# Attention stage: the mixer gates' steps given out two at a time, six matmuls of 512 columns in a row instead of three

## The chip, the core and the metric

The kernel runs on one core of a Trainium2 chip. The core has five engines with a queue of instructions each: TensorE (PE in the profile, with its weight loads shown apart as PEld), VectorE (DVE), ScalarE (ACT), GpSimd (POOL) and SyncE (SP), which starts most of the DMAs. Operands lie in the on-chip memory SBUF, matmul results in PSUM, which has eight banks of 512 float32 columns on 128 partitions. The metric is device time in microseconds (us) from start to end of one execution.

## The reference

One layer of a decoder trunk with two token mixers side by side, whose outputs are weighed by gates; 1024 tokens of 1024 values, float32.

```python
h = rmsnorm(x, norm_mix[layer])
(q, kc, vc, ks, vs, kw, vw, nsa_g, rq, rk, rv, rg, gate_a, gate_b) = jnp.split(
    h @ w_in[layer], offsets, axis=-1)
...
nsa_out = nsa_batched(q, kc, vc, ks, vs, kw, vw, nsa_g.reshape(B, S, NSA_HEADS, 3), ...)
ret_out = (jax.nn.silu(rg.astype(jnp.float32)) * ret.reshape(B, S, RET_W)).astype(x.dtype)
mix = (jax.nn.sigmoid(gate_a) * (nsa_out @ w_proj_a[layer])
       + jax.nn.sigmoid(gate_b) * (ret_out @ w_proj_b[layer]))
x = x + mix @ w_out[layer]
h = rmsnorm(x, norm_mlp[layer])
x = x + jnp.square(jax.nn.relu(h @ w_up[layer])) @ w_down[layer]
return rmsnorm(x, norm_final)
```

`nsa_mixer` is the attention: 8 query heads in 2 groups, and three branches for each query block of 128 tokens (compressed keys, selected blocks of 64 keys, all 16 of which are taken at this length, and a window of 512 keys), each with a softmax of its own and summed with gates.

## The kernel before

The kernel goes through stages: norm and projections, retention, attention, output projection, MLP. The change lies in the attention stage, 357 to 742 us of the trace. The order of PE's instructions there is written by hand: PE runs them as the program gives them. The order on the other engines is made by a scheduler in the framework, from the program's order and what each instruction needs; only instructions marked with `keep_in_program_order` are held to it.

A float32 product is made of three matmuls: each operand is split into a high part (`wh`, `QQ`, `ph`; on ACT) and the rest (`wl`, `ql`, `pl`; a subtraction on DVE), and high by high, low by high and high by low are added up in PSUM.

The stage has 32 units: query blocks 7 down to 0, two groups each, two pairs of heads each. A unit's work is given out by generators, one piece at each call:

- `scores` (L1105 on): for each of the two heads the matmuls of the scores S over the selected keys (`KKs`), then over the window (`KKw`) with the compressed ones. Each group of up to 512 columns takes one of the four banks of the pool `psS`. DVE adds the mask and takes the extreme value `mx` (L1152, L1159), ACT the exponent (L1163) from the bank into `pSa`, `pSb` or `pW`, and then the bank is free. DVE makes the factors `cf` (L1168 to L1170) and POOL scales the weights (L1173).
- `pv`: for two blocks of keys at a time four transposes (L1232, L1233) into a `pt` bank, `ph` on ACT (L1234), `pl` on DVE (L1235), and, two groups later, the matmuls into O (`V`), with a bank of its own.
- `prep_q`: splits the next queries (L1097, L1098).

Between these lie the mixer gates (`gate_a`, `gate_b`): 32 half rows, made by `gate_pieces`. Each is eight steps of three matmuls of 512 columns (`gps<-bh,wh`, `gps<-bl,wh`, `gps<-bh,wl`) into one bank, with a `yield` behind each step; then ACT takes the bank (`gst`, L1059) and SP writes it out. At the sixth step `gate_w(i + 1)` asks for the next weight, once for two half rows: a DMA into `raw`, `wh` on ACT (L185) and `wl` on DVE (L188), 1024 columns each. The gps bank is one; from the seventeenth half row on every second one takes a bank of the pool of the scores instead.

What stands where is decided by a list of places. `place(it, n, lo, hi)` gives `n` pieces of a generator the midpoints of `n` equal parts of `lo` to `hi`, in units; the list is sorted by these numbers and run through. For the gates:

```python
        for n, k in enumerate(GATES):
            place(gate_it, k, n - 1, n)
```

`GATES` has the number of steps in each unit: 14, then 8 in sixteen units, 6 in twelve, 7 in the last four; together 242, and two more (`GATE0`) ahead of the first. The remaining 12 of the 256 steps come behind the stage.

Of the kernel before, what the change touches and what calls it, by code (L numbers as in the profile page):

```python
# [37 lines left out]
PH_B = 4  # L38
PS_B = 4
PS_S = 4  # L40
GATES = [14] + [8] * 16 + [6] * 12 + [7, 7, 7, 7]
S_BEG = 0.08
S_END = 0.6
W_AT = 0.7
# [69 lines left out]
def hybrid_block(ctx: ExitStack, tc: tile.TileContext, a: dict, out: bass.AP):  # L114
# [954 lines left out]
    def all_gates():  # L1069
        for n in range(32):  # L1070
            yield from gate_pieces(n)

    gate_it = all_gates()

    def gates(k=1):
        for _ in range(k):
            next(gate_it, None)

    with ExitStack() as e3:
# [13 lines left out]
        def prep_q(qb, g):  # L1093
            qt = qs[qb, g]
            QQ = at.tile([P, 4, P], F32R, name="QQ")
            ql = at.tile([P, 4, P], F32R, name="ql")
            A.activation(QQ, qt, AF.Copy)  # L1097
            V.tensor_sub(ql, qt, QQ)  # L1098
            qs[qb, g] = (QQ, ql)
            nxt = 2 * (7 - qb) + g + 2  # L1100
            if nxt < 16:
                load_q(7 - nxt // 2, nxt % 2)
            yield
# [150 lines left out]
        def n_scores(qb):  # L1254
            sel, win = (qb + 4) // 4, (min(qb + 1, 5) + 3) // 4 + (1 if qb == 3 else 0)
            return 2 * (sel + win)

        def n_pv(qb):
            return 2 * ((qb + 1 + min(qb + 1, 5) + 2) // 2)
# [9 lines left out]
        def place(it, n, lo, hi):  # L1269
            for k in range(n):  # L1270
                todo.append((lo + (hi - lo) * (k + 0.5) / n, len(todo), it))

        for n, (qb, g, hp) in enumerate(units):
            u = {}
            if hp == 0:
                if n:
                    place(prep_q(qb, g), 1, n - 1 + Q_AT - 1, n - 1 + Q_AT - 1)
            if n % 4 == 0:
                todo.append((n - 1 + S_BEG, len(todo), None, qb))
            it = scores(qb, g, hp, u)  # L1280
            ahead = SHORT if qb < 2 else 0.0
            place(it, n_scores(qb), n - 1 + S_BEG - ahead, n - 1 + S_END - ahead)
            place(it, 1, n - 1 + W_AT - ahead, n - 1 + W_AT - ahead)
            it = pv(qb, g, hp, u)
            place(it, n_pv(qb) - 1, n, n + 1 + V_END)
            last = 1.1 / n_pv(units[n + 1][0]) if n + 1 < nu else V_LAST
            place(it, 1, n + 1 + last, n + 1 + last)
        for n, k in enumerate(GATES):
            place(gate_it, k, n - 1, n)
        gates(GATE0)  # L1290
        next(prep_q(7, 0))
        todo.append((B_AT, len(todo), None, None))
# [754 lines left out]
```

## Time and profile before

| | |
|---|---|
| median of 3 runs | 1544.56 us (1544.07 to 1545.82) |
| profiled execution: span from first to last instruction | 1542.0 us |
| instructions in the span | 22621 |
| PE / DVE / ACT / POOL busy, of the span | 99% / 68% / 47% / 33% |
| chain of waits, share of PE | 89% |
| attention stage | 357 to 742 us |

The profile gives the span of one execution; the runs' time also has what lies ahead of the first and behind the last instruction, 2.6 us by the median. A row of a timeline has the start, the duration in us, the engine, the line, the operation and what it writes and reads, without the numbers of the buffers; in square brackets stands the idle time before it and what released it. The view by lines has the number, the busy time, the mean of one in ns and the idle time before. In the waits each row has the waiting and the releasing instruction, the us in all, the number of times and the longest.

### The profile page before, as it was taken

What the parts mean: (1) busy time and instruction counts of PE and PEld (TensorE: products, weight loads), DVE (VectorE), ACT (ScalarE), POOL (GpSimd) and SP (SyncE); (2) the same over time, 40 slices, a digit from 0 to 9 for tenths busy, and PEclk for the clock granted to TensorE, in tenths of its full rate; (3) what the DMA queues carried; (4) which work ended last, traced back from release to release, by engine and by line L of the source; (5) the groups of instructions that cost most, each with busy time, mean ns of one, the idle gap of its engine ahead of it and who ended that gap; (6) DMA issues with size and microseconds to landing.
All of it is one profiled execution on the core that took longest, in us unless ns stands there. A gap on an engine that the chain in (4) does not pass through costs nothing.

```text
span 1542.0 us, 22621 instructions
## 1 busy us (share of the span) xinstructions
PE 1529.9 (99%) x7841; PEld 1290.3 (84%) x7841; DVE 1044.4 (68%) x2044; ACT 719.1 (47%) x1602; POOL 514.3 (33%) x601
## 2 busy tenths in 40 slices
PE   9999999999999999999999999999999999999998
PEld 6888888898888888888888888888888888888887
DVE  6865661666877878776754378876666768786573
ACT  6653462555677777776421163222222244443452
POOL 4110011002333333343000014767777518723540
PEclk9999999999999999999999999999999999999999
DMA  6202215762111212111744433444444797673472
GB/s 208 88 18 65 59 45 131 204 177 68 58 35 42 62 42 62 48 56 62 233 137 157 137 126 104 154 151 150 150 150 150 242 344 265 207 238 123 143 269 100
DMA packets 101764, 202.87 MB, mean 132 GB/s; under 512 B 10698, under 2 KB 27346, under 8 KB 101586
## 3 DMA queue, kind: packets, MB, share of 16 engines
q1 hardware_dynamic: 100946, 199.33, 39.9%
q0 software_dynamic: 560, 1.84, 0.3%
q8 instruction: 62, 1.02, 0.3%
q14 instruction: 52, 0.43, 0.1%
q10 hardware_dynamic: 144, 0.26, 0.0%
HBM read 147.78 MB, written 53.61 MB: 131 GB/s over the span
## 4 chain that ended last, share of the span: by engine, by line
PE 89%; DVE 4%; issue 3%; ACT 2%; POOL 1%; DMA 1%; POOLq 0%; SPq 0%; ACTq 0%; DVEq 0%
PE mm L158 24%; PE mmu L158 20%; PE mmd L158 19%; PE gps L158 10%; PE S L158 4%; PE O L158 4%; PE pt L1233 2%; PE pt L1232 2%; PE pc L158 1%; PE pO L158 1%; ACT pW L1163 1%; PE pD L158 0%; PE tp L391 0%; PE pS L158 0%; DVE pl L1235 0%
## 5 line engine op out<-in xcount | busy, mean ns | idle before, releaser
L1387 DVE TENSOR_TENSOR wl<-raw,wh 128x1024 fp32r<-128x1024 f32 x134 | 220.5, 1670 | 91.3 <-ACT wh L1386 91.3
L1386 ACT ACTIVATE wh<-raw 128x1024 fp32r<-128x1024 f32 x134 | 136.7, 1054 | 159.4 <-PE mmd L158 112.3
L158 PE MATMUL mmd<-wl,wh 128*128 128x512 f32 (+1 forms) x464 | 177.2, 382 | 0.0
L158 PE MATMUL mmd<-wh 128*128 128x512 f32 (+1 forms) x464 | 177.2, 382 | 0.0
L158 PE MATMUL mmd<-wh,wl 128*128 128x512 f32 (+1 forms) x464 | 177.1, 382 | 0.0
L194 POOL TENSOR_SCALAR msq<-ssq 128x1 f32<-128x1 f32 (+1 forms) x32 | 7.5, 234 | 384.3 <-ACT h L200 219.6
L1235 DVE TENSOR_TENSOR pl<-pt,ph 128x512 fp32r<-128x512 f32 (+1 forms) x160 | 103.4, 648 | 40.4 <-ACT ph L1234 38.9
L158 PE MATMUL mm<-wh,bh 128*128 128x512 f32 (+1 forms) x320 | 122.4, 383 | 0.1
L158 PE MATMUL mm<-wl,bh 128*128 128x512 f32 (+1 forms) x320 | 118.9, 372 | 0.0
L158 PE MATMUL mm<-wh,bl 128*128 128x512 f32 (+1 forms) x320 | 118.0, 373 | 0.0
L1234 ACT ACTIVATE ph<-pt 128x512 fp32r<-128x512 f32 (+1 forms) x160 | 90.9, 569 | 54.0 <-PE pt L1233 53.0
L1152 DVE CUSTOM_DVE_ANT_0 S<-S,edge_m 128x352 f32<-128x352 f32 (+5 forms) x200 | 101.4, 514 | 13.9 <-PE S L158 10.3
L158 PE MATMUL gps<-bh,wh 128*128 128x512 f32 x256 | 107.8, 421 | 0.7 <-ACT gst L1059 0.6
L158 PEld LDWEIGHTS mmd<-wh 128*128 128x128 f32 x464 | 87.2, 188 | 17.1
L158 PEld LDWEIGHTS mmd<-wl,wh 128*128 128x128 f32 x464 | 87.2, 188 | 17.0
L158 PEld LDWEIGHTS mmd<-wh,wl 128*128 128x128 f32 x464 | 87.2, 188 | 16.7
L158 PE MATMUL mmu<-bh,wh 128*128 128x512 f32 (+1 forms) x264 | 101.0, 383 | 0.0
L158 PE MATMUL mmu<-bl,wh 128*128 128x512 f32 (+1 forms) x264 | 100.9, 383 | 0.0
L158 PE MATMUL mmu<-bh,wl 128*128 128x512 f32 (+1 forms) x264 | 100.6, 383 | 0.0
L158 PE MATMUL gps<-bl,wh 128*128 128x512 f32 x256 | 100.6, 393 | 0.0
L158 PE MATMUL gps<-bh,wl 128*128 128x512 f32 x256 | 100.5, 393 | 0.0
L1173 POOL TENSOR_SCALAR pSa<-pSa,cf 128x512 f32<-128x512 f32 (+3 forms) x64 | 38.9, 621 | 173.4 <-DVE mx L1159 63.5
(379 smaller groups left out, 4161.9 us busy)
## 6 DMA issues: line engine op xcount, KB each, us to landing
raw<-u_scr SPq DMA_DIRECT2D x56, 512.0 KB, 4.3
raw<-w_down SPq DMA_DIRECT2D x41, 512.0 KB, 5.1
raw<-w_up SPq DMA_DIRECT2D x32, 512.0 KB, 4.0
u_scr<-u SPq DMA_DIRECT2D x60, 256.0 KB, 4.2
u_scr<-s SPq DMA_DIRECT2D x45, 256.0 KB, 2.3
y<-w_down SPq DMA_DIRECT2D x16, 512.0 KB, 6.6
x<-x SPq DMA_DIRECT2D x8, 512.0 KB, 4.8
raw<-w_ga SPq DMA_DIRECT2D x8, 512.0 KB, 3.8
```

The source lines that it names most:

```text
L158: T.matmul(o, w, m, start=start, stop=stop)
L194: G.tensor_scalar(m[:, :w], ssq, 1.0 / n, EPS, op0=OP.mult, op1=OP.add)
L1152: r = V.tensor_tensor_reduce(sc, sc, mk, -0.125, BIGPOS, OP.add, OP.min, mx[:, i, b:b + 1])
L1163: A.activation(o, sc, AF.Exp, bias=mx[:, i, m:m + 1], scale=-1.0, accum_out=sums[:, i, b:b + 1])
L1173: G.tensor_scalar(v, v, cf[:, i, b:b + 1], 1.0, op0=OP.mult, op1=OP.mult)
L1232: T.transpose(tp[:, bi * 2], p0, ident)
L1233: T.transpose(tp[:, bi * 2 + 1], p1, ident)
L1234: A.activation(ph[:, :n], tp[:, :n], AF.Copy)
L1235: V.tensor_sub(pl[:, :n], tp[:, :n], ph[:, :n])
L1386: A.activation(h[:, :n], r, AF.Copy)
L1387: V.tensor_sub(l[:, :n], r, h[:, :n])
```

## The change

The gates' steps are given out two at a time. A new generator calls `gates(2)` for each piece, and half as many pieces are placed in each unit, so that each is six matmuls of 512 columns in a row, and there are half as many of them. For that the counts have to be even, and the last four of `GATES` become 8, 6, 8, 6; the sum stays 242.

```diff
-GATES = [14] + [8] * 16 + [6] * 12 + [7, 7, 7, 7]
+GATES = [14] + [8] * 16 + [6] * 12 + [8, 6, 8, 6]
...
+        def gate_rows():
+            while True:
+                gates(2)
+                yield
+
+        rows_it = gate_rows()
         for n, k in enumerate(GATES):
-            place(gate_it, k, n - 1, n)
+            place(rows_it, k // 2, n - 1, n)
```

What this moves on PE, in a unit of query block 5 behind the scores of the second head (the gap between the first head's selected score and the first window score `S<-KKw,QQ` has this piece and the like one of the head before in it):

```order
 L158 MATMUL S<-KKs,QQ 128x256
 L158 MATMUL S<-KKs,ql 128x256
-L158 MATMUL gps<-bh,wh 128x512
-L158 MATMUL gps<-bl,wh 128x512
-L158 MATMUL gps<-bh,wl 128x512
 L158 MATMUL O<-ph,VV 128x256
 L158 MATMUL O<-pl,VV 64x256 x2
```

The step that stood between the last selected score and the O matmuls is gone from there. It is now part of a row of six behind the first window score:

```order
 L158 MATMUL S<-KKw,QQ 128x352
 L158 MATMUL S<-KKw,ql 128x352
+L158 MATMUL gps<-bh,wh 128x512
+L158 MATMUL gps<-bl,wh 128x512
+L158 MATMUL gps<-bh,wl 128x512
+L158 MATMUL gps<-bh,wh 128x512
+L158 MATMUL gps<-bl,wh 128x512
+L158 MATMUL gps<-bh,wl 128x512
 L1232 MATMUL pt<-ident,pW 128x128
 L1233 MATMUL pt<-ident,pW 128x128
```

On DVE, at the end of a unit of query block 6 in which a gate weight is split (442 to 449 us of the trace of before), the rows before are:

```order
L1098 TENSOR_TENSOR ql_5512<-qt_4710,QQ_5511 128x512
L1168 TENSOR_TENSOR sums_4947<-sums_4947 128x2
L1169 RECIPROCAL cf_4949<-sums_4947 128x2x2
L1170 TENSOR_TENSOR cf_4949<-cf_4949,gts_89 128x2x2
L1235 TENSOR_TENSOR pl_5075<-pt_5073,ph_5074 128x512
L188 TENSOR_TENSOR wl_5088<-raw_5085,wh_5087 128x1024
L1235 TENSOR_TENSOR pl_5107<-pt_5105,ph_5106 128x256
L1235 TENSOR_TENSOR pl_5136<-pt_5134,ph_5135 128x512
```

and now, at the same place:

```order
L1235 TENSOR_TENSOR pl_5050<-pt_5048,ph_5049 128x512
L1168 TENSOR_TENSOR sums_4943<-sums_4943 128x2
L1169 RECIPROCAL cf_4945<-sums_4943 128x2x2
L1170 TENSOR_TENSOR cf_4945<-cf_4945,gts_89 128x2x2
L188 TENSOR_TENSOR wl_5079<-raw_5076,wh_5078 128x1024
L1235 TENSOR_TENSOR pl_5084<-pt_5082,ph_5083 128x512
L1235 TENSOR_TENSOR pl_5104<-pt_5102,ph_5103 128x256
L1098 TENSOR_TENSOR ql_5518<-qt_4716,QQ_5517 128x512
```

The subtraction of the gate weight, `wl`, has moved ahead of the second but last `pl` of the unit (`pl_5075` before, `pl_5084` now; the last one is of 256 columns), and the split of the next queries, `ql`, from before the factors to behind the last `pl`. On PE the consumers stand in this order now:

```order
L158 MATMUL gps_4961<-bh_85,wh_4670 128x512
L158 MATMUL gps_4961<-bl_86,wh_4670 128x512
L158 MATMUL gps_4961<-bh_85,wl_4671 128x512
L158 MATMUL O_4925<-pl_5050,VV_3667 64x256
L158 MATMUL O_4925<-ph_5049,VV_3667 128x256
L158 MATMUL O_4925<-pl_5050,VV_3667 64x256
L158 MATMUL O_4925<-ph_5049,VV_3667 128x256
L158 MATMUL O_4925<-pl_5084,VV_3667 64x256
L158 MATMUL O_4925<-ph_5083,VV_3667 128x256
```

The O matmuls of `pl_5084` follow those of `pl_5050` without a gate step between them; before, a step lay between these two groups of four.

## The prediction

> **What bounds the kernel now.** I read the page first, then the waits of the attention stage on TensorE, then the timeline of two places in it. The busy row, the slices and the row of clocks come first.
>
> ```profile
> PE 1529.9 (99%) x7841; PEld 1290.3 (84%) x7841; DVE 1044.4 (68%) x2044; ACT 719.1 (47%) x1602; POOL 514.3 (33%) x601
> PE   9999999999999999999999999999999999999998
> PEclk9999999999999999999999999999999999999999
> core 0: 1542.0 us, clock 0.999
> ```
>
> TensorE (PE) works from the first slice to the last, at a granted clock of 0.999, so the end is set by how much PE has to do and by the gaps in it. The view by stretches, for the attention stage alone (its columns: span, then busy time and instructions of PE, PEld, DVE, ACT and POOL, granted clock, DMA share and GB/s):
>
> ```profile
> 357.00:742.00 385.00, 382.46 (x2356) 331.84 (x2355) 292.69 (x1025) 274.02 (x796) 132.42 (x284) 1.00 0.19 59
> ```
>
> PE is busy for 382.46 of 385.00 us; VectorE (DVE) 292.69 and ScalarE (ACT) 274.02. Nothing that comes from a higher clock can be had here, and little from gaps. The waits of the weight loads (PEld) in that window, which stand for PE's, with us, times and the longest:
>
> ```profile
> PEld O L158 <- DVE pl L1235: 3.0, 5, 0.9
> PEld gps L158 <- ACT gst L1059: 1.4, 3, 0.6
> PEld S L158 <- ACT pW L1163: 1.3, 2, 0.8
> PEld S L158 <- ACT pSa L1163: 0.8, 2, 0.5
> PEld S L158 <- ACT pSb L1163: 0.2, 1, 0.2
> ```
>
> All of it is 3.0 + 1.4 + 1.3 + 0.8 + 0.2 = **6.7 us**. That is the most that a better order could give back from waits, 0.43% of 1542.0.
>
> **The work itself.** The change moves steps and adds none: 242 steps of three matmuls before and after. So the sum has one term for the matmuls' own time and three for waits. The gate matmuls by kind:
>
> ```profile
> L158 PE MATMUL gps<-bh,wh 128*128 128x512 f32 x256 | 107.8, 421 | 0.7 <-ACT gst L1059 0.6
> L158 PE MATMUL gps<-bl,wh 128*128 128x512 f32 x256 | 100.6, 393 | 0.0
> ```
>
> The first of three lasts 421 ns, the second 393, so a row of six might seem to save 28 ns in each pair. But most of that is overlap: the timeline below has starts at 494.36, 494.59 and 494.82, 0.23 us apart for the first matmul after another kind as for the second. I cost the switch at **0**; were all 28 ns real, 121 pairs would give back 3.4 us (that is the low bound, and a rival below). Nothing speaks for a loss above 0.
>
> **Term 1, the score banks.** Four banks hold the scores S, and the first window score of a unit takes the bank of the first selected score of that unit. It must wait until ACT has taken the exponent of that one. A unit of query block 5 in the timeline (start, duration):
>
> ```profile
> 494.24 0.28 PE L158 MATMUL S<-KKs,ql 128*128 128x256 f32 x1
> 494.36 0.40 PE L158 MATMUL gps<-bh,wh 128*128 128x512 f32 x1
> 494.59 0.39 PE L158 MATMUL gps<-bl,wh 128*128 128x512 f32 x1
> 494.82 0.39 PE L158 MATMUL gps<-bh,wl 128*128 128x512 f32 x1
> 495.04 0.69 DVE L1235 TENSOR_TENSOR pl<-pt,ph 128x512 fp32r<-128x512 f32 x1
> 495.64 0.42 DVE L1152 CUSTOM_DVE_ANT_0 S<-S,edge_m 128x256 f32<-128x256 f32 x1
> 495.98 0.14 DVE L1152 DVE_READ_ACCUMULATOR2_ANT mx<- 128x1 f32 x1
> 496.16 0.16 DVE L1159 TENSOR_TENSOR mx<-mx 128x1 f32<-128x1 f32 x1
> 496.41 0.69 ACT L1163 ACTIVATE pSa<-S,mx 128x512 f32<-128x512 f32 x1
> 497.34 0.33 PE L158 MATMUL S<-KKw,QQ 128*128 128x352 f32 x1
> ```
>
> The next matmul starts at 494.36, the window score at 497.34: PE has 2.98 us of other work between them, and the exponent (496.41 + 0.69 = 497.10) is done in time, by 0.24 us. In that gap stand two gate steps, six matmuls of 0.23 us = 1.38 us. The order of the changed kernel takes both out of it (they now stand before the selected score and behind the window score), so 2.98 − 1.38 = **1.60 us** are left. The same order has three such units in query block 5 and four in query block 4. One of those four:
>
> ```profile
> 535.32 0.28 PE L158 MATMUL S<-KKs,ql 128*128 128x256 f32 x1
> 537.26 0.58 ACT L1163 ACTIVATE pSa<-S,mx 128x384 f32<-128x384 f32 x1
> 538.32 0.33 PE L158 MATMUL S<-KKw,QQ 128*128 128x352 f32 x1
> ```
>
> The gap is 538.32 − 535.32 − 0.12 = 2.88 there, and 1.50 is left. The chain on the other side, from the score's end (0.2 us for its tail): the maximum 0.42 + 0.14, then one pl 0.69, which DVE's order puts ahead of mx, mx 0.16, about 0.1 of hand-over, the exponent 0.69 (0.58 in block 4). That is 2.4 us (2.3). The stall is 2.4 − 1.6 = 0.8; I take 0.75 in each of seven units, **+5.3 us**. If DVE does mx before pl becomes ready, it is 0.4 each (+2.8); if the chain is as long as in the rows (497.10 − 494.36 = 2.74) and also the units of blocks 6 and 7, whose gap is now 2.2, stall by 0.5, it is 7 × 1.15 + 8 × 0.5 = 12. In the last query blocks the present kernel has such waits already:
>
> ```profile
> 626.90 0.40 PE L158 MATMUL S<-KKw,QQ 128*128 128x288 f32 x1 [0.53 <-ACT pW L1163]
> ```
>
> They are the 1.3 + 0.8 + 0.2 = 2.3 us above. The new order has other short distances there (1.2 to 1.7 us, three places); I put what goes and what comes at the same 2.3, net **0**, within ±1.5.
>
> **Term 2, the ends of the units with a new gate weight.** Every second unit, eight in all, a gate weight is split: wh on ACT, wl on DVE, between the exponents and the last pl of that unit. The place in the present kernel:
>
> ```profile
> 442.14 0.32 PE L158 MATMUL S<-KKw,ql 128*128 128x352 f32 x1
> 443.49 0.17 DVE L1159 TENSOR_TENSOR mx<-mx 128x1 f32<-128x1 f32 x1
> 443.95 0.56 ACT L1163 ACTIVATE pW<-S,mx 128x352 f32<-128x352 f32 x1
> 444.48 0.51 ACT L1163 ACTIVATE pW<-S,mx 128x288 f32<-128x288 f32 x1
> 444.95 0.33 ACT L1163 ACTIVATE pW<-S,mx 128x64 f32<-128x64 f32 x1
> 445.72 1.09 ACT L185 ACTIVATE wh<-raw 128x1024 fp32r<-128x1024 f32 x1
> 445.96 3.12 POOL L1173 TENSOR_SCALAR pW<-pW,cf 128x640 f32<-128x640 f32 x4 [0.32 <-ACT ph L1234]
> 446.84 1.76 DVE L188 TENSOR_TENSOR wl<-raw,wh 128x1024 fp32r<-128x1024 f32 x1 [0.25 <-ACT wh L185]
> 448.53 1.01 DVE L1235 TENSOR_TENSOR pl<-pt,ph 128x256 fp32r<-128x256 f32 x2
> 448.99 0.33 PE L158 MATMUL O<-pl,Vc 128*64 128x256 f32 x1 [0.41 <-DVE pl L1235]
> ```
>
> Here one pl stands behind wl on DVE, and PE waits 0.41 us for it (the longest of the five such waits is 0.9). In the changed order wl goes ahead of two pl's, the first of which is wanted earlier. PE's way from the start of the last window score to that O, by starts (0.17 a score, 0.117 an O, 0.109 a transpose, 0.23 a gate matmul): 0.17 + 0.47 + 1.38 + 0.44 + 0.47 + 0.22 + 1.38 + 0.47 = 5.0 us; in the other units 4.8 to 5.5. The way over the others, on the rows' durations: the rows have mx at 443.49 behind a pl, which now comes after it, so I take 1.3 us to mx, 1.7 for the three exponents with their read-outs, 1.1 for wh, 1.76 for wl, 0.69 for pl, sum 6.55 us; with the short wl below, 6.0. The stalls by units are then, from short to long: 0.8–1.35 and 1.0–1.5 (two units each), 0.35–0.9 and 0.3–0.8 (two each), in sum 4.9 to 9.1. I take **8.0**, near the top, since POOL's scaling starts from the same exponents and so lies beside wl. The present 3.0 us of this wait go, so the net is **+5.0** (+1.9 to +6.1).
>
> The length of wl has two prices in this stage, one beside POOL's scaling and one with POOL idle:
>
> ```profile
> 358.56 1.23 DVE L188 TENSOR_TENSOR wl<-raw,wh 128x1024 fp32r<-128x1024 f32 x1 [0.44 <-ACT wh L185]
> 490.84 2.16 POOL L1173 TENSOR_SCALAR pW<-pW,cf 128x640 f32<-128x640 f32 x4 [0.30 <-DVE cf L1170]
> ```
>
> The scaling took 3.12 beside wl and 2.16 without it, wl 1.76 beside it and 1.23 without it: both lose. The Trainium skill, page "SBUF — State Buffer", section "Who interferes with whom", says that "a DVE instruction with two SBUF inputs contends with a GpSimd instruction that reads SBUF"; this trace agrees (1.76 against 1.23 us). By the rule the long wl is right for all eight units; without it 8 × 0.53 = 4.2 us of term 2 would fall away, and the total would be 1549.3.
>
> **Term 3, the gate's eviction.** The next gate's first matmul waits for ACT to empty the one gps bank. With steps in pairs the distance between one gate's last matmul and the next gate's first is no longer 0.9 us but 2.0 to 2.75 us of other work, since the end of a gate always ends a pair. The 1.4 us go: **−1.4** (none gone: 0). That no step is paid twice in DMA follows from its count being unchanged.
>
> **Sum.** 0 + 5.3 + 0 + 5.0 − 1.4 = +8.9 us on the profiled span, 1542.0 → 1550.9. The median of the runs, 1544.56, is 2.6 us over the span, time before its first and after its last instruction, which the change does not touch: 1553.5 us, 0.58% slower. The low ends (2.8 + 1.9 − 1.4 − 1.5) give +1.8, the high ends (12 + 6.1 + 1.5 − 0) +19.6.
>
> **Rivals.** A difference of 0.2%, 3.1 us, is about what a measurement of this kernel can tell from none.
>
> (a) Faster. The row of six lets ACT and DVE catch up, and the chains of term 1 and 2 get shorter than the distances: the S chain under 1.5 us, which decides it, and wl back to 1.23 with wh taken before the exponents. Then no new wait comes and the old ones go: all 6.7 us of them (1537.9), or the 3.4 us of the switches with the 1.4 of the evictions (1539.8); I put it at 1539. For it speaks that DVE is idle for 92 us in the stage; against it that every duration in the chain is a row and their sum is 2.3. Chance 0.09.
>
> (b) No difference. Chains of 1.9 and 5.4 us, with short stalls of 0.3 in seven and 0.3 in eight units: 2.1 + 2.4 − 3.0 − 1.4 = 0.1, so 1544.6. It speaks for this that a stall in one place gives the other engines time, so that the next one in the same unit is shorter. Chance 0.15. That the order does not change is not to be had: the order of the changed kernel shows the pairs.
>
> (c) Worse. The longer chains of the rows (2.74) hold also in blocks 6 and 7, term 1 is 12 and term 2 at 6: 1544.6 + 16.6 = 1561. Chance 0.18.
>
> The forecast has 0.58. **Chances**: faster 0.09, within 0.2% 0.15, slower 0.58 + 0.18 = 0.76. The range goes from 1545.5 (part of (b), above the low sum's half) to 1561.5; outside lie (a), half of (b) and the tail of (c).
>
> **What would show it.** In the profile after: waits of S for ACT's pSa, seven or so of 0.75 us in query blocks 5 and 4 (term 1); waits of O for pl, about eight of 1 us, each behind a wl of 1.7 us (term 2); no wait of gps for gst (term 3); the sum of PE's busy time in the stage as before but for the overlap of ends. It would be wrong if the first window score of those seven units starts without a wait, or if wl no longer stands ahead in time of the last pl's.

## The result and the profile after

The changed kernel took 1560.72 us (1560.47 to 1561.00, 4 runs), the kernel before 1544.32 us beside it (1543.45 to 1545.82, 4 runs). The ratio of the runs is 1.0113, with a 95% interval of 1.0101 to 1.0125: slower by 1.1%. The prediction had 1553.5 us, slower by 0.6%, with a range to 1561.5; the ratio times the median it was made against, 1544.56, is 1562.0, just outside. The direction was right, the size about half.

The page of the changed kernel: its span, the busy row and the granted clock by slices:

```profile
span 1559.0 us, 22606 instructions
...
PE 1532.7 (98%) x7841; PEld 1295.3 (83%) x7841; DVE 1048.2 (67%) x2044; ACT 717.3 (46%) x1602; POOL 521.5 (33%) x601
...
PEclk9999999999999999999999999999999999999999
```

The span has grown by 17.0 us (the runs' medians by 16.4), PE's busy time by 2.8, the number of matmuls and the clock not at all. So PE waits. Where, the view by stretches shows (the columns are as in the prediction), the attention stage up to 600 us and the rest of it, to 760:

```profile
357.00:600.00 243.00, 230.55 (x1427) 201.90 (x1426) 185.58 (x626) 166.19 (x473) 85.65 (x157) 1.00 0.16 49
600.00:760.00 160.00, 155.83 (x932) 134.77 (x932) 112.27 (x400) 106.58 (x323) 51.09 (x128) 1.00 0.20 66
```

In the first stretch PE has 12.5 us without work, in the second 4.2; the whole stage of before had 2.5. The weight loads' waits in the changed kernel, first 357 to 600 us, then 600 to 760 us:

```profile
PEld O L158 <- DVE pl L1235: 10.3, 9, 1.7
PEld S L158 <- ACT pSa L1163: 5.8, 8, 1.0
PEld pt L1232 <- ACT gst L1059: 0.2, 1, 0.2
```

```profile
PEld O L158 <- DVE pl L1235: 1.4, 2, 1.0
PEld S L158 <- ACT pW L1163: 1.4, 2, 1.1
PEld gps L158 <- ACT pSa L1163: 1.4, 2, 1.0
PEld S L158 <- ACT pSa L1163: 0.8, 1, 0.8
PEld pt L1232 <- issue: 0.7, 1, 0.7
PEld S L158 <- ACT gst L1059: 0.5, 1, 0.5
```

Two rows of 0.2 us are left out at the end. The same view of before, 357 to 600 us:

```profile
PEld O L158 <- DVE pl L1235: 2.7, 4, 0.9
PEld gps L158 <- ACT gst L1059: 1.4, 3, 0.6
PEld S L158 <- ACT pSa L1163: 0.2, 1, 0.2
PEld S L158 <- ACT pSb L1163: 0.2, 1, 0.2
```

After 600 us before had what is left of the 6.7 us that the prediction quotes, 2.1 by the rows of that stretch (1.3 + 0.5 for scores, 0.3 for O). The account, in the prediction's terms:

| term | before | after | net | predicted net |
|---|---|---|---|---|
| 1: scores wait for their bank, to 600 us | 0.4 | 5.8 | +5.4 | +5.3 |
| 2: O waits for pl, to 600 us | 2.7 | 10.3 | +7.6 | +5.0 |
| 3: waits for a gate's eviction | 1.4 | 0.2 | −1.2 | −1.4 |
| late units, from 600 us on, all waits | 2.1 | 6.6 | +4.5 | 0 |
| sum | 6.6 | 22.9 | +16.3 | +8.9 |

These rows explain 16.3 of 17.0 us. Term 1 in the trace, at the second of the three units of query block 5 that have it:

```profile
512.24 0.28 PE L158 MATMUL S<-KKs,ql 128*128 128x256 f32 x1
512.56 0.43 DVE L1152 CUSTOM_DVE_ANT_0 S<-S,edge_m 128x256 f32<-128x256 f32 x1 [0.82 <-PE S L158]
513.01 0.69 DVE L1235 TENSOR_TENSOR pl<-pt,ph 128x512 fp32r<-128x512 f32 x1
513.62 0.15 DVE L1159 TENSOR_TENSOR mx<-mx 128x1 f32<-128x1 f32 x1
513.86 0.69 ACT L1163 ACTIVATE pSa<-S,mx 128x512 f32<-128x512 f32 x1 [0.27 <-DVE mx L1159]
514.69 0.43 PE L158 MATMUL S<-KKw,QQ 128*128 128x352 f32 x1 [0.57 <-ACT pSa L1163]
```

The next matmul behind the first row (a transpose) started at 512.36. From there the chain is mask, pl, mx, exponent, to 514.55: 2.19 us, and with the hand-over 2.33 to the window score. The matmuls between the two need 1.60. The difference is 0.73, the score's real delay; the bracket shows 0.57 of it, since it counts from the modelled end of the matmul before. All seven units have it (0.50 to 0.84 in brackets).

Term 2, at the end of the first unit of block 5 that splits a gate weight:

```profile
502.02 0.33 PE L158 MATMUL S<-KKw,ql 128*128 128x352 f32 x1
502.78 0.56 ACT L1163 ACTIVATE pW<-S,mx 128x352 f32<-128x352 f32 x1
504.79 0.56 ACT L1163 ACTIVATE pW<-S,mx 128x352 f32<-128x352 f32 x1
506.10 1.06 ACT L185 ACTIVATE wh<-raw 128x1024 fp32r<-128x1024 f32 x1
506.79 3.12 POOL L1173 TENSOR_SCALAR pW<-pW,cf 128x640 f32<-128x640 f32 x4 [1.51 <-DVE cf L1170]
507.19 1.47 DVE L188 TENSOR_TENSOR wl<-raw,wh 128x1024 fp32r<-128x1024 f32 x1 [0.57 <-ACT wh L185]
508.58 1.28 DVE L1235 TENSOR_TENSOR pl<-pt,ph 128x512 fp32r<-128x512 f32 x2
509.32 0.33 PE L158 MATMUL O<-pl,VV 128*64 128x256 f32 x1 [1.50 <-DVE pl L1235]
```

Last score, exponents until 506.10, wh, wl, pl, O: the chain that was predicted, but 4.08 us long up to wh, where the prediction had 3.0. In block 6, by the same view, it is 2.73, and the wait there 1.10:

```profile
441.03 0.56 ACT L1163 ACTIVATE pW<-S,mx 128x352 f32<-128x352 f32 x1 [0.16 <-DVE mx L1159]
441.38 0.32 PE L158 MATMUL S<-KKw,ql 128*128 128x352 f32 x1
442.81 0.57 ACT L1163 ACTIVATE pW<-S,mx 128x352 f32<-128x352 f32 x1
444.11 1.09 ACT L185 ACTIVATE wh<-raw 128x1024 fp32r<-128x1024 f32 x1
447.62 0.33 PE L158 MATMUL O<-pl,VV 128*64 128x256 f32 x1 [1.10 <-DVE pl L1235]
```

Of the window's exponents each fence has the first of three of each head. In block 5 both heads' exponents, six in all, lie between the last window score and wh. In block 6 the first head's begin 0.35 us ahead of that score, so the second head's begin 1.43 us behind it, and not 2.77. It is so in all eight units: up to wh it is 4.08 and 4.09 us in block 5, 3.80 in both units of block 4, and 2.67 to 2.76 in blocks 7 and 6.

### The profile page after: what moved, and what is told of

Its sections match the earlier page's. It is cut to its first block, busy times and chain, and to the rows that moved or that the text cites. A ratio compares the mean times of both kernels' runs of the same rounds, so it can differ in the third digit from the quotient of the medians.

```text
span 1559.0 us, 22606 instructions
## 1 busy us (share of the span) xinstructions
PE 1532.7 (98%) x7841; PEld 1295.3 (83%) x7841; DVE 1048.2 (67%) x2044; ACT 717.3 (46%) x1602; POOL 521.5 (33%) x601
## 4 chain that ended last, share of the span: by engine, by line
PE 85%; DVE 5%; ACT 4%; issue 3%; POOL 1%; DMA 1%; SPq 0%; POOLq 0%; ACTq 0%; DVEq 0%
PE mm L158 23%; PE mmu L158 21%; PE mmd L158 19%; PE gps L158 9%; PE S L158 3%; PE O L158 3%; ACT pW L1163 2%; PE pt L1232 1%; PE pt L1233 1%; DVE pl L1235 1%; DVE wl L188 1%; PE pc L158 1%; DVE S L1152 1%; PE pO L158 1%; ACT wh L185 1%
```

## The experiments

Times are medians; each ratio is against the kernel before in the same session (1544.32 us for the changed kernel, 1543.1 to 1543.8 for the others). The span is that of the profiled run, to be held against 1559.0 of the changed kernel and 1542.0 of the kernel before. The two columns of waits are the weight loads' over the stage.

| kernel | us | ratio (95%) | span | O for pl | S for pSa |
|---|---|---|---|---|---|
| changed | 1560.72 | 1.0113 (1.0101 to 1.0125) | 1559.0 | 11.7 | 6.6 |
| weight split earlier | 1551.41 | 1.0053 (1.0038 to 1.0068) | 1549.7 | 1.7 | 6.6 |
| rows 1/16 unit later | 1553.18 | 1.0065 (1.0050 to 1.0080) | 1551.0 | 5.3 | 4.9 |
| units 9 to 15 single | 1549.14 | 1.0039 (1.0025 to 1.0054) | 1546.6 | 5.4 | 1.0 |
| without wl | 1551.50 | 1.0054 (1.0039 to 1.0069) | 1549.8 | 3.6 | 6.6 |
| without any split | 1548.12 | 1.0033 (1.0021 to 1.0045) | 1547.1 | 0.7 | 6.3 |
| pairs in 9 to 15 alone | 1554.57 | 1.0073 (1.0058 to 1.0088) | 1552.7 | 8.9 | 6.4 |
| pairs from 16 on alone | 1547.84 | 1.0030 (1.0018 to 1.0042) | 1545.9 | 4.2 | 1.1 |
| pairs in 0 to 8 alone | 1544.35 | 1.0008 (0.9998 to 1.0017) | 1542.6 | 4.0 | 0.7 |
| second row ahead | 1553.28 | 1.0065 (1.0049 to 1.0080) | 1552.5 | 9.3 | 2.1 |
| second row ahead, late split | 1542.01 | 0.9992 (0.9983 to 1.0001) | 1540.0 | 0.9 | 2.1 |
| QQ held | 1572.04 (one run) | | 1570.3 | 12.2 | 6.7 |
| late pairs, one gate bank | 1546.02 | 1.0014 (1.0004 to 1.0023) | 1544.4 | 3.6 | 0.2 |

**Is it wl that makes O wait?** The weight asked for two steps earlier, all else as in the changed kernel:

```diff
-            if k == 5:
+            if k == 3:
                 gate_w(i + 1)
```

> The changed kernel, but the next gate weight is asked for at the fourth step of a gate instead of the sixth, so that wh and wl stand half a unit earlier, among the window scores and not at the unit's end; PE's order is that of the changed kernel. Theory 1 (PE waits for O at the ends of the units because wl stands ahead of two pl's on DVE): the O waits, 11.7 us in the changed kernel, fall to 3 or less, the score waits (6.6 for pSa) stay within 1 us, time about 1552 (1550 to 1554). Theory 2 (the rows of six themselves leave DVE late, and wl is only one of many things on it): the waits come back at other places, time 1558 or more.

O's waits are down to two, and the score waits are untouched:

```profile
PEld S L158 <- ACT pSa L1163: 6.6, 9, 1.0
PEld O L158 <- DVE pl L1235: 1.7, 2, 1.3
```

The span fell by 9.3 us. PE's order is the same, so the rows of six do not make these waits by themselves; the place of the split does.

**Without wl, and without any split.** In the first, the low part of the gate weights from the third on isn't made, and the high part is used in its place; in the second, these weights are neither loaded nor split:

```diff
-            gw[i] = split_w(a[src][:, ii], (KD, P), pool=wring, pin=i > 1)
+            if i < 2:
...
+            gw[i] = (h, h)
...
-            gw[i] = split_w(a[src][:, ii], (KD, P), pool=wring, pin=i > 1)
+            gw[i] = split_w(a[src][:, ii], (KD, P), pool=wring, pin=i > 1) if i < 2 else gw[1]
```

> The changed kernel with the subtraction wl of the gate weights from the third on left out: their high part is used in place of the low part, so the gates lack their correction; PE's instructions are as many and as long. Theory 1 (wl stands in the chain of the last pl's): each O wait behind a wl, 0.5 to 1.75 us, falls by up to the 1.5 us that wl takes, in sum from 11.7 to 2 or 3, time about 1552. Theory 2 (the last masks and the splitting of the queries are late by themselves, and wl only follows them): the O waits fall by 4 us at most, time 1556 or more.

> The changed kernel with the gate weights from the third on neither loaded nor split: the second one is used for all later gates, so ACT has no wh and DVE no wl in the stage; PE's instructions are as many and as long. Theory 1 (the chain at a unit's end is exponents, wh, then wl on DVE and ph behind wh on ACT; with wl alone gone 3.6 us of O waits were left): these fall below 1.2, time about 1549 (a further 2.4 below the kernel without wl, 1551.5). Theory 2 (what was left is the splitting of the next queries, QQ and ql, ahead of the last exponents): 3 us or more of O waits stay, time 1551 or more.

Without wl 3.6 us of O waits are left, a little above the 2 or 3 expected; without any split 0.7. What holds them in the first is seen at the same unit end, in the timeline of the kernel without wl (wh stands at L1039 there, and the later line numbers are six higher):

```profile
502.58 1.06 ACT L1039 ACTIVATE wh<-raw 128x1024 fp32r<-128x1024 f32 x1
503.27 2.17 POOL L1179 TENSOR_SCALAR pW<-pW,cf 128x640 f32<-128x640 f32 x4 [1.53 <-DVE cf L1176]
503.53 0.60 ACT L1240 ACTIVATE ph<-pt 128x512 fp32r<-128x512 f32 x1
504.16 0.69 DVE L1241 TENSOR_TENSOR pl<-pt,ph 128x512 fp32r<-128x512 f32 x1 [1.05 <-ACT ph L1240]
504.90 0.33 PE L158 MATMUL O<-pl,VV 128*64 128x256 f32 x1 [0.62 <-DVE pl L1241]
```

DVE now sits idle (1.05 us) for a ph that stands behind wh on ACT. So of the O waits of 11.7 us about 8 hang on wl and 3 more on wh, with its load; the rest of the stage makes 0.7. The scaling on POOL takes 2.17 us here and took 3.12 beside wl, which is the contention that the prediction priced.

**Distance against chain for the scores.** Every row of six a sixteenth of a unit later, which puts one into the gap between the selected and the window scores:

```diff
-            place(rows_it, k // 2, n - 1, n)
+            place(rows_it, k // 2, n - 1 + 0.5 / k, n + 0.5 / k)
```

> The changed kernel with every row of six placed one sixteenth of a unit later, so that in query blocks 5 and 4 one row stands again between the first head's selected scores and the first window score. Theory 1 (the score waits come from the distance on PE, 1.6 us against a chain of 2.3): the seven waits of 0.7 to 1.0 us (5.3 in all) go, time at most 1555.4, less if the O waits shrink too. Theory 2 (a row of six brings a score wait wherever it stands, since it takes ACT and DVE out of step): the score waits stay at 5 us or more, time 1559 or more.

Neither expectation held whole: the time, 1553.18, is that of theory 1, but half of the score waits stayed (0.33 to 0.53 by the starts, where they had been 0.66 to 1.0). The chain at the same unit of block 5:

```profile
508.07 0.28 PE L158 MATMUL S<-KKs,ql 128*128 128x256 f32 x1
509.99 0.16 DVE L1159 TENSOR_TENSOR mx<-mx 128x1 f32<-128x1 f32 x1
510.22 0.60 ACT L1234 ACTIVATE ph<-pt 128x512 fp32r<-128x512 f32 x1 [1.41 <-PE pt L1233]
510.71 0.68 ACT L1163 ACTIVATE pSa<-S,mx 128x512 f32<-128x512 f32 x1
511.54 0.43 PE L158 MATMUL S<-KKw,QQ 128*128 128x352 f32 x1 [0.19 <-ACT pSa L1163]
```

The row of six has pushed the next transposes back, from 508.19 to 509.58, and the ph that they feed stands ahead of the exponent on ACT: mx was there at 510.15, the exponent began at 510.71. The distance had grown to 3.0 us, and the chain with it, from 2.33 to 3.35 (508.19 to 511.54). This kernel moves every row of the stage, so its time is not the price of these seven waits alone. To change the distance alone, only the second row of each unit with four rows was moved, from 0.375 to 0.365:

```diff
+            if k == 8 and True:
+                for w in (0.125, 0.365, 0.625, 0.875):
+                    place(rows_it, 1, n - 1 + w, n - 1 + w)
+            else:
+                place(rows_it, k // 2, n - 1, n)
```

> The changed kernel with the second of the four rows of six in a unit (units 1 to 16) placed at 0.365 of the unit instead of 0.375, that is, just ahead of the O matmuls before the first window score and not behind that score; nothing else moves in the list. The distance from the first head's selected scores to the first window score is 1.60 + 1.38 = 2.98 us again, and the transposes ahead of it stay where they are, so ACT's and DVE's chain should keep its 2.3 us. Theory 1 (distance against chain): the seven score waits of 0.66 to 1.0 us (5.3) go altogether, the O waits lose some more, time 1559.5 - 5.3 or a little lower, 1551 to 1554.5. Theory 2 (as in the kernel with rows placed a sixteenth later, where half of these waits stayed: the chain grows with whatever stands in it): 2 us or more of them stay, 1556 or more.

(The row lands behind those O matmuls, directly ahead of the window score; the distance is the same.) The first window score now starts 0.23 to 0.24 us behind the last matmul of the row in all seven units, so the seven waits, 5.3 us in all, are gone. The view of the waits:

```profile
PEld O L158 <- DVE pl L1235: 9.3, 10, 1.4
PEld S L158 <- ACT pSa L1163: 2.1, 7, 0.8
```

The 2.1 us that are left are others: 0.85 at 634 us, as in the changed kernel, and six of 0.17 to 0.32, of which PE's starts show 0.19 at most. The time, 1553.28, is as expected. O's waits, though, moved both ways. By starts they fell in blocks 5 and 4 (from 1.4 to 1.75 each to between 0.46 and 0.76), where wl now begins 2.4 to 3.8 us behind the last window score and not 4.9 to 5.2. They rose in the two such units of block 7, from about 0.5 to 1.3, where wl took 1.77 and 1.70 us and not 1.22 and 1.23.

**Does each unit pay for itself?** Single steps in the units 9 to 15 of the changed kernel, and then pairs in one part of the units only (the same edit with the condition `not 9 <= n <= 15`, `n < 16` or `n > 8` for the single steps):

```diff
-            place(rows_it, k // 2, n - 1, n)
+            if 9 <= n <= 15:
+                place(gate_it, k, n - 1, n)
+            else:
+                place(rows_it, k // 2, n - 1, n)
```

> The changed kernel with the steps given out singly again in the units 9 to 15 (query blocks 5 and 4 but for their first unit) and in pairs elsewhere. Theory 1 (each wait belongs to its unit): the seven score waits (5.3) and the four long O waits there (1.75, 1.75, 1.37, 1.44, together 6.3) go, some 0.8 of the old gate waits come back: 1560.7 - 5.3 - 6.3 + 0.8 = 1550, within 1.5. Theory 2 (what is lost in one place is won back or lost again in the next): less than half of it goes, 1555 or more.

> Steps in pairs in the units 9 to 15 alone, singly elsewhere. Theory 1 (each unit pays for its own pairs, the parts add up): what giving them out singly there saved, 1559.0 - 1546.6 = 12.4 us by the spans, is what they cost: about 1543.1 + 12 = 1555 (1553.5 to 1556.5), with seven score waits of 0.7 to 1.0 us and four O waits of 1.4 to 1.8. Theory 2 (the loss is made by the rows before and after): 1550 or less.

> Steps in pairs from the unit 16 on (query blocks 3 to 0), singly before. Theory 1: the late waits of the changed kernel from 606 us on (1.03, 0.94, 0.36, 0.80, 0.50, 0.50, 0.35 for banks and 0.42, 1.00 for pl, together 5.9) in place of the 2.4 of the kernel before: +3.5, about 1546.6 (1545.5 to 1548). The prediction's own term for this part was 0, within 1.5: 1543.1 (1541.6 to 1544.6).

> Steps in pairs in the units 0 to 8 (query blocks 7 and 6, and one unit of 5), singly after. Theory 1: the changed kernel has there 3.5 us of O waits and some 0.8 of short score waits, in place of 1.6 of O waits and 1.4 to 1.7 of gate waits: +1, about 1544.1 (1543 to 1545.5). Theory 2, the prediction's high end (score waits of 0.5 in each of these units): +4 or more, 1547.

By the spans, pairs cost 10.7 us in the units 9 to 15, 3.9 from 16 on and 0.6 up to 8, in sum 15.2 of the 17.0; taking them away in 9 to 15 gave back 12.4. By the medians of the runs, each against the kernel before beside it, it is 11.5, 4.8 and 1.3, in sum 17.5 of 16.4, and 10.4 given back. Both ways the parts add up within 2 us, so little is lost or won back in other units. The late part, for which the prediction had 0, is 3.9 (4.8). The early part, with a ratio of 0.9998 to 1.0017, can't be told from none.

**What makes the late waits?** From the seventeenth gate half on every second gate takes one of the four score banks for its eight steps. Late pairs again, with all gates in the one gate bank:

```diff
-GALT = 17
+GALT = 99
```

> Pairs from unit 16 on as in the run with the late pairs alone, and every gate takes the one gps bank, none a bank of the scores. Theory 1 (the late waits come from five users of four score banks at a shorter distance): the waits of scores and gates for pSa, pW and gst there, 1.4 + 1.0 + 1.1 + 0.5 = 4.0 us in the run with the late pairs, fall under 1; waits of gates for gst come in their place, of up to 0.9 us each at the odd ends of gates, 2 to 3 us in all; time 1546 to 1548. Theory 2 (the distances between scores alone make them, as in blocks 5 and 4): 2 us or more of score waits stay, time 1549 or more.

From 590 us on, no score waits are left; gates wait for their eviction instead (two rows at the transposes, 0.7 and 0.2 us, are left out):

```profile
PEld gps L158 <- ACT gst L1059: 2.6, 5, 1.2
PEld O L158 <- DVE pl L1235: 0.9, 2, 0.5
```

The span fell by 1.5 us against late pairs with the shared banks (1545.9 to 1544.4). So the late score waits need the gates among the score banks' users, but 2.4 us of loss stay (1544.4 against 1542.0). The same setting with single steps was not tried.

**QQ ahead of the exponents.** In the unit ends of block 5 the next queries' split stands ahead of the window's exponents on ACT, in block 6 it doesn't; that could explain 4.08 us up to wh against 2.73. It was held to the program's order:

```diff
-            A.activation(QQ, qt, AF.Copy)
+            tc.keep_in_program_order(A.activation(QQ, qt, AF.Copy))
```

> The changed kernel with QQ, the split of the next queries on ACT (0.63 us), held to the program's order, which puts it behind the last exponents and wh at the end of the first unit of query block 5 that splits a gate weight; in the changed kernel it stands ahead of the window's exponents there, and the O wait behind wl was 1.75 us. Read at this place alone, since the hold also moves ACT's and DVE's order elsewhere and can cost time there (score waits for queries that come late). Theory 1 (QQ on ACT delays the exponents, and with them wh, wl and pl): the O wait there falls to 1.3 us or less, as in the units of block 6, where QQ stands behind wh already (1.26). Theory 2 (ACT has slack there, the wait is set by DVE): 1.6 or more.

```profile
503.10 0.56 ACT L1163 ACTIVATE pW<-S,mx 128x352 f32<-128x352 f32 x1 [1.18 <-DVE mx L1159]
507.31 1.76 DVE L188 TENSOR_TENSOR wl<-raw,wh 128x1024 fp32r<-128x1024 f32 x1 [0.26 <-ACT wh L185]
508.08 0.68 ACT L1097 ACTIVATE QQ<-qt 128x512 fp32r<-128x512 f32 x1
509.72 0.33 PE L158 MATMUL O<-pl,VV 128*64 128x256 f32 x1 [1.50 <-DVE pl L1235]
```

QQ has gone behind wh, and the wait at this place is the same 1.50 us. Theory 1 falls. ACT now waits 1.18 us for mx instead: the first head's exponents begin 0.77 us behind the last window score, where they began 0.76 behind it with QQ ahead of them. From that score to wh it is 3.85 us and not 4.08, but wl takes 1.76 us beside POOL's scaling and not 1.47. So in block 5 it is mx that holds the exponents. Whether that comes late by the place of the scores on PE or by the masks and a pl on DVE, no run isolates; this stays open. Elsewhere the hold costs much, in waits for queries that come late (5.7 us for ql, 3.0 for QQ).

**A version without the three terms.** The second row ahead of the window score, single steps from unit 16 on, and the next weight asked for at the eighth step (`k == 7`), behind the last pl's:

> Pairs in the units 0 to 15 with the second row ahead of the first window score as in the run before, single steps from unit 16 on, and the next gate weight asked for at the eighth step instead of the sixth, behind the last pl's of the unit. By theory 1 all three terms of the loss are gone (seven score waits, the O waits behind wl, the late banks), and of the kernel before's waits the gates' 1.4 and the O waits' 1.6 are gone too: 1543.1 - 3.0 + about 1 for short score waits in the first units = 1541 (1539.5 to 1543). If something else than these waits made the loss, 1545 or more.

```profile
PEld S L158 <- ACT pSa L1163: 2.1, 7, 0.5
PEld S L158 <- ACT pW L1163: 1.5, 2, 0.8
PEld O L158 <- DVE pl L1235: 0.9, 1, 0.9
```

With rows of six in sixteen units it takes 1542.01 us beside 1543.17; the interval, 0.9983 to 1.0001, just holds no difference. The weight loads' waits are 4.7 us in all, where the kernel before has 6.7. So in these units the pairs show no cost of their own: what the change lost there lies in what it moved past what. The kernel before with the late split alone was not run, so a small cost of the pairs could be hidden by what that split gains.

## Why the prediction went as it did

- **Bound, clock, matmuls.** Right: the number of matmuls and the clock are the same. The first matmul of a step lasts 409 ns in the mean where it lasted 421, but the starts in a row of six stay 0.23 us apart, and no run shows a gain from it. The switch between kinds at 0 held.
- **Term 1, +5.3 us.** Right in place, count and size: seven units, six with 0.66 to 0.73 us by the starts and one with 1.00, in sum 5.3, where 0.75 each was taken, by the very order mask, pl, mx, exponent; the move of one row out of the gap made the waits, and a row put back undid them. The 0.5 us for each unit of blocks 7 and 6 in the high bound did not come.
- **Term 2, +5.0 us.** Right in mechanism (0.7 us of O waits are left without the split), too small: +7.6. The step that failed is "I take 1.3 us to mx, 1.7 for the three exponents", one chain for all eight units, taken from one place in block 6. It held in block 6 (2.73 us up to wh against 3.0; the waits are 1.26 by the starts, inside the stated 1.0 to 1.5). In blocks 5 and 4, where the way over PE is longer (5.3 to 5.6 us against 5.0), the stalls were put at 0.3 to 0.9; by the starts they are 1.75, 1.75, 1.37 and 1.44, since six exponents, and not three, stand behind the last window score there, and the chain up to wh was 4.1 us in block 5 and 3.8 in block 4. In the first two units, put at 0.8 to 1.35, the stalls are 0.5. The listed stalls also don't follow from the stated ways of 4.8 to 5.5 us, which against 6.0 and 6.55 would give 0.5 to 1.75; they fit ways of about 5.05 to 5.75.
- **The price of wl.** "The long wl is right for all eight units" was wrong for six of them. In block 7 wl began 0.25 and 0.06 us ahead of POOL's scaling and took 1.22 and 1.23, while the scaling took 3.44 and 3.63; in block 6 it began 0.13 and 0.09 behind it and took 1.74 and 1.78; in blocks 5 and 4 it began 0.40 behind it and took 1.47 each time. The eight took 11.85 us, where 8 × 1.76 is 14.1. This term was too large, then, and hid a part of what the exponents lacked.
- **Term 3, −1.4 us.** Right: no gate waits for its eviction in the changed kernel up to 600 us; one transpose behind it does, for 0.2 us.
- **Late units, 0 within 1.5.** Wrong, and the larger failure: "I put what goes and what comes at the same 2.3". After 600 us the waits for score banks are 3.6 us (1.4 + 1.4 + 0.8) in place of 1.8. On top come 1.4 us of O waits in place of 0.3 (1.0 of it behind a wl again, at 657 us), 0.7 of issue, 0.5 for a gate's eviction and twice 0.2: +4.5, by the run with late pairs alone +3.9. That sum was not worked out from distances as term 1 was, though they were at hand.
- **Sum and range.** Of the 7.4 us between +8.9 and +16.3, the late units make 4.5 and term 2 makes 2.6. The prediction's own high ends add up to +19.6, 1564.2 us, but its range stopped at 1561.5. The 17.0 us lie inside that sum only because the high end of term 1, which did not come, is 6.7 above its value; term 2 and the late units each went past their own bounds. The 2.6 us between span and run set the median against another execution; in the later runs it is 1.7 to 2.1 us for the profiled execution itself, so the medians moved by 16.4 where the spans moved by 17.0.
- **Rivals.** (a), the engines catch up, did not happen: pairs in no part of the units saved time. (b) needed chains of 1.9 and 5.4 us; they are 2.33 and 5.7 to 7.3 (from the last window score to O). (c), 1561, has the right number by luck: its score waits in blocks 7 and 6 are not there, and it had nothing for the late units.
- **The page on SBUF.** The Trainium skill, "SBUF — State Buffer", section "Who interferes with whom", says that "a DVE instruction with two SBUF inputs contends with a GpSimd instruction that reads SBUF"; this agreed again, now from the other side. The four scalings took 2.17 us with wl left out and 3.12 with it, at the same place.

## What to carry to other kernels

When work is given out in larger pieces on an engine that is always busy, price the gaps it leaves: for each buffer that comes free through other engines, hold the work that stands between the two uses against the chain that frees it, unit by unit, the quiet end of the stage included. A chain read at one place is a price for that place; where the neighbours on ACT and DVE differ, read it again. And look at what else hangs on the moved piece: here a request for the next weight rode on it, and the waits behind its split grew by more (7.6 us up to 600) than those for the score banks (5.4).

## What the runs showed that was not expected

- Moving a row of matmuls into a gap lengthened the chain that the gap was to cover: the transposes behind the row came 1.39 us later, and ACT did their ph (510.22) ahead of the exponent (510.71), though mx was there at 510.15. About half of the waits stayed.
- An instruction taken out of a chain ahead of wl (QQ, 0.63 us) brought nothing at O: wh began only 0.23 us earlier, and wl then took 1.76 us beside POOL's scaling where it had taken 1.47.
